# Two decoder layers on one core: one shared pool of buffers, PSUM banks returned earlier, activation tables asked for early, memory keys after the output projection

## The chip, the core and the metric

The kernel runs on one core of one Trainium2 chip. The metric is the device time of one execution in microseconds (us). An engine is named as the profile does: PE is TensorE's matmul side and PEld its weight loads, DVE is VectorE, ACT is ScalarE, POOL is GpSimd, SP is SyncE, which here only issues DMAs.

## What is computed

The reference is a trunk of two decoder layers over 256 tokens of width 1024, in float32. Each layer adds three things to the residual stream x:

```python
x = x + mixer(rms_norm(x, norm_mix[i]), ...)
x = x + memory_cross_attention(rms_norm(x, norm_mem[i]), rms_norm(mem, norm_mem_src[i]), ...)
x = x + swiglu(rms_norm(x, norm_ffn[i]), ffn_w_in[i], ffn_w_out[i])
```

Layer 0's mixer has two groups of eight heads: A selects the top 64 keys of every query by a small indexer, B attends to all causal keys of its block. Layer 1's mixer has 16 heads in 4 groups and three branches (compressed blocks, selected blocks, a window), mixed by gates. Both end in an output projection of 1024 columns. The memory attention has 4 heads of 128 dimensions over 256 memory tokens; its keys are `m @ w_k` of the normed memory and depend on no token of the trunk. The feed-forward part has 2816 hidden columns.

## The kernel before

The 256 tokens are two tiles (t = 0 and 1) of 128 partitions. A float32 product is made of three matmuls in the fp32r format: the operand and the weight are each split into a high part and a rest (`mm3`, L571), so a product over K blocks of 128 rows is 3 K matmuls of up to 512 columns. A weight arrives in units of 256 rows by 512 columns (512 KB) by DMA into one of 3 `raw` buffers; `pusher` (L401) writes its high part (`move`, on ACT or DVE) and its rest (DVE) into one of 6 `whl` buffers, in the fixed order of `plan` (L423 to L444). Each unit serves both token tiles and is then free.

The program has no fixed order of instructions. When it is built, some dozens of generator threads offer instructions, and a list scheduler (`Steps.run`, L108) always issues the one that can start first by its own estimate of the engines' clocks (`Est`, L141), ties within 0.03 us going to the lower rank. So the order on every engine is set at build time by estimated costs, by ranks and by free buffers. A buffer class is a `Slots` object (L269): a thread that wants a buffer waits until one is open. Before the change these classes are separate: 23 `slab`, 4 `t2`, 3 `sn`, 4 `pt`, 2 `gv` (each buffer 2 KB per partition), 2 `t4`, and in PSUM two banks each of `mm`, `sp`, `tp` and `po`.

One thread, `main` (L1502, rank 4, the last in a tie), issues all large products (`gemm`, L577) one after the other: the mixer's input projections, then `mem_k` (L1290, the memory's keys, 48 matmuls), then `project` (L1398, the output projection, 96 matmuls: half 0 for tiles 0 and 1, then half 1), then `mem_attn` (L1315), then `ffn`. Each `gemm` takes one of the two `mm` banks and hands it to an evacuation thread. Most of these call `inv_rms` (L655): ACT squares the bank into a `t2` buffer, DVE sums, POOL takes the inverse root; the caller gives the bank back after that. The attention threads (`attention`, `scores`, L699) run beside `main` at rank 2: two matmuls into an `sp` bank, a masked minimum on DVE into an `sn` buffer, exponentials on ACT, a scaling on POOL or DVE, four transposes into a `tp` bank, a copy into `pt`, and the products with the values into a `po` bank. When a group of eight heads is done for a tile, `finish` (L760) copies it from `po` into two slabs (rows named `slab<-po`), and `project` may use it: it waits for `("oT", t, half)`. `mem_prep` (L1263, rank 2) loads the memory, transposes it and writes it into 8 slabs (rows `slab<-gv`) behind the last projections of the mixer; `mem_k` waits for it.

So what covers the attention's chains on PE is whatever `main` may issue meanwhile. In layer 0 that is the values' projection (`bv`), `mem_k` and `project`; in layer 1 the last query projections, `mem_k` and `project`.

The order of `main` for each layer, before:

```python
            yield from (mixer0 if L == 0 else mixer1)()
            yield from mem_k(L)
            ver += 2
            for t in range(NT):
                spawn(norm(("mem", L), t, 16 + 8 * L, ver))
            yield from project(L)
```

Of the kernel before, what the change touches and what calls it, by code (L numbers as in the profile page):

```python
# [8 lines left out]
F32 = mybir.dt.float32  # L9
# [6 lines left out]
P = 128  # L16
# [37 lines left out]
NSLAB = 23  # L54
TAPS = 8
PTS = 4


class Op:
# [17 lines left out]
    def issue(self):  # L77
        e, outs, ins, cost, f = self.best()[2]
        self.est.issue(e, outs, ins, cost)
        f()  # L80
        for op in self.then:
            op.issue()
# [58 lines left out]
class Est:  # L141


    def __init__(self, nc):
        self.clk = {"PE": 0.0, "V": 0.0, "S": 0.0, "G": 0.0, "D": 0.0, "port": 0.0}
        self.wr, self.rd, self.busy = {}, {}, {}
        self.thin = False
        self.now = 0.0
# [46 lines left out]

    def issue(self, e, outs, ins, cost):
        lock = self.locks(e, outs, ins)
        t = max(self.clk[e], self.after(e, outs, ins), self.clk["port"] if lock else 0.0)
        if e == "PE":
            w = int(t / 3.413)  # L200
            c = cost * (1 if self.busy.get(w - 1, 0.0) > 1.26 else 2)
            n = 1
            for d in outs[0].shape[1:]:
                n *= d
            self.busy[w] = self.busy.get(w, 0.0) + cost * ins[0].shape[0] / P * min(1.0, n / P)
# [14 lines left out]
    class Engine:  # L220
# [3 lines left out]
        def __getattr__(self, name):  # L224
            f = getattr(self.e, name)

            def call(*a, **k):
# [9 lines left out]
                def do():  # L237
                    return f(*a, **{q: v() if q in ("start", "stop") and callable(v) else v for q, v in k.items()})  # L238
                return Op(self.est, [(self.n, outs, ins, self.cost(name, a, k, outs, ins), do)])
            return call  # L240

        def cost(self, name, a, k, outs, ins):
# [56 lines left out]

@with_exitstack  # L300
def trunk(ctx: ExitStack, tc: tile.TileContext, I, out):
# [37 lines left out]
    spawn = ck.spawn  # L339
    MM, SP, TP, PV = Slots(est, pp, "mm", 2), Slots(est, pp, "sp", 2), Slots(est, pp, "tp", 2), Slots(est, pp, "po", 2)  # L340
    SL = Slots(est, hp, "slab", NSLAB)
    T2, T4, SN, PT = Slots(est, tp, "t2", 4), Slots(est, tp, "t4", 2), Slots(est, tp, "sn", 3), Slots(est, tp, "pt", PTS)
    RP = Slots(est, tp, "rope", 3)
    GV = Slots(est, tp, "gv", 2)
# [127 lines left out]
    PO.memset(one, 1.0).issue()  # L472
    mhalf = cp.tile([P, 16], F32, name="mhalf")
# [18 lines left out]
    def tables():  # L492
# [20 lines left out]
        yield S.activation(cos, ang, AF.Sin)  # L513
        yield has(("mix0", 0), 2)
# [254 lines left out]
    def mixer0():  # L769
# [100 lines left out]
        def ev_q(j, key):  # L870
            def ev(ps, free, t):
                q, qf = yield from T2.get([P, 8, HD])
                yield move(q.rearrange("p h d -> p (h d)"), ps)
                yield from inv_rms(ps, 8, HD, (yield from root("mix0", t))[0], 1.0, HD, rq[j, t])
                free()
# [13 lines left out]
        def ev_k(ps, free, t):  # L889
# [3 lines left out]
            yield from inv_rms(ps, 8, HD, (yield from root("mix0", t))[0], 1.0 / HD, 1.0, rk)  # L893
            free()
# [75 lines left out]
        spawn(mem_prep(0), 2)  # L970
# [22 lines left out]
    def mixer1():  # L993
# [92 lines left out]
        def ev_sw(br):  # L1086
            def ev(ps, free, t):
# [4 lines left out]
                yield from inv_rms(ps[:, :256], G, HD, v, 1.0 / HD, 1.0, rk[:, :G])  # L1092
                if br == 0:
                    yield S.activation(vv[:, t, :G, :], ps[:, 256:].rearrange("p (h d) -> p h d", h=G), AF.Copy, scale=r)
                free()
# [28 lines left out]
        def ev_q(j):  # L1124
            def ev(ps, free, t):
                q, qf = yield from T2.get([P, 8, HD])
                yield move(q.rearrange("p h d -> p (h d)"), ps)
                yield from inv_rms(ps, 8, HD, (yield from root("mix1", t))[0], 1.0, HD, rq[j, t])
                free()
# [128 lines left out]
        spawn(mem_prep(1), 2)  # L1258
# [31 lines left out]
    def mem_k(L):  # L1290
# [3 lines left out]
        def ev(ps, free, t):  # L1294
# [3 lines left out]
            yield from inv_rms(ps, MH, MD, mvr[t][0], 1.0 / MD, 1.0, rk)  # L1298
            free()
# [15 lines left out]
    def mem_attn(L):  # L1315
        vm = hp.tile([P, NT, MH, MD], F32, name="mvm")
        qT, rq = {}, [hp.tile([P, MH], F32, name=f"mrq{t}") for t in range(NT)]

        def ev_q(ps, free, t):
            q, qf = yield from T2.get([P, MH, MD])  # L1320
            yield S.activation(q.rearrange("p h d -> p (h d)"), ps, AF.Copy)
            yield from inv_rms(ps, MH, MD, (yield from root(("mem", L), t))[0], 1.0, MD, rq[t])
            free()
# [20 lines left out]
        def mem_pv(t, p, sp, spf, sn, snf):  # L1344
# [20 lines left out]
            for i in range(2):  # L1365
                yield together([T.matmul(po[:, i, :], vm[:, b, h0 + i, :], pt[:, 2 * i + b, :], start=(b == 0), stop=(b == 1))
                                for b in range(2)])
            ptf()
# [191 lines left out]
```

## Time and profile before

| what | us |
|---|---|
| median of 3 runs | 803.68 |
| lowest and highest run | 800.99, 805.22 |
| the profiled execution, its own time | 802.33 |
| its span, from first to last instruction | 800.6 |
| PE busy in the span | 765.6 |
| DVE, ACT, POOL busy | 533.0, 436.7, 132.8 |

The profiled execution's own time is 1.7 us over its span, and 1.35 us under the median. A PE that is shown busy is not always at full rate: a matmul's record reaches over the start of the next, so short waits between matmuls are hidden in it. Line numbers in the trace are all L238, the helper that records every instruction; the rows are told apart by their tiles. `whl` are split weights, `mm`, `sp`, `tp`, `po` the PSUM banks, `t` the buffers of `t2` and `t4`.

### The profile page before, as it was taken

How to read it: one execution, taken by the hardware profiler on the slowest of the kernel's cores; microseconds unless marked ns; L12 is line 12 of the kernel's file. 1: busy time of each engine (PE TensorE's matmuls, PEld its weight loads, DVE VectorE, ACT ScalarE, POOL GpSimd, SP SyncE). 2: the span in 40 equal slices, each digit the busy share in tenths (PEclk: the TensorE clock that was granted, in tenths of full speed). 3: DMA queues.
4: the chain of work that ended last, by engine and by line, in shares of the span. 5: the costliest groups of instructions: out<-in, count | busy, mean ns of one | idle time of the engine just before them, and what ended most of it. 6: DMA issues, size and time to landing. Idle time of an engine off the chain costs nothing.

```text
span 800.6 us, 11834 instructions
## 1 busy us (share of the span) xinstructions
PE 765.6 (96%) x4259; PEld 635.5 (79%) x4259; DVE 533.0 (67%) x1088; ACT 436.7 (55%) x822; POOL 132.8 (17%) x194
## 2 busy tenths in 40 slices
PE   6988999999999999999998988999999999999998
PEld 5766788897888889788877767887897888889886
DVE  6888998868555554554726888886857565546541
ACT  5766985675543443443615677884656344435430
POOL 1665340100000000000016373340200000000000
PEclk9998999999999999999999998999999999999999
DMA  7633643426556645876414623033624665546751
GB/s 221 192 98 92 194 136 100 142 102 193 166 171 206 186 156 157 228 247 186 131 46 123 212 78 106 2 105 108 188 102 132 211 187 183 160 140 212 218 189 52
DMA packets 69482, 121.27 MB, mean 151 GB/s; under 512 B 8420, under 2 KB 15664, under 8 KB 69424
## 3 DMA queue, kind: packets, MB, share of 16 engines
q1 hardware_dynamic: 69392, 120.53, 48.8%
q8 instruction: 33, 0.54, 0.3%
q14 instruction: 25, 0.20, 0.1%
q0 software_dynamic: 32, 0.00, 0.0%
HBM read 119.46 MB, written 1.05 MB: 151 GB/s over the span
## 4 chain that ended last, share of the span: by engine, by line
PE 78%; DVE 8%; ACT 5%; DMA 5%; issue 2%; POOL 1%; SPq 0%; ACTq 0%; DVEq 0%; POOLq 0%
PE mm L238 58%; PE po L238 11%; PE tp L238 7%; PE sp L238 2%; DVE whl L238 2%; DVE slab L238 1%; ACT whl L238 1%; DMA raw<-in_ffn_w_in 1%; DMA raw<-in_ab_w_in 1%; ACT sn L238 1%; DMA raw<-in_nsa_w_in 1%; ACT slab L238 1%; DVE sn L238 1%; DVE kvT L238 1%; DVE hss L238 1%
## 5 line engine op out<-in xcount | busy, mean ns | idle before, releaser
L238 PE MATMUL mm<-whl,h 128*128 128x512 f32 (+3 forms) x1776 | 399.1, 379 | 10.1 <-DVE whl L238 9.1
L238 PEld LDWEIGHTS mm<-whl,h 128*128 128x128 f32 x1776 | 311.8, 189 | 69.9 <-DVE whl L238 10.9
L238 DVE TENSOR_TENSOR whl<-raw,whl 128x1024 fp32r<-128x1024 f32 (+3 forms) x232 | 271.3, 1174 | 143.3 <-ACT whl L238 139.0
L238 ACT ACTIVATE whl<-raw 128x1024 fp32r<-128x1024 f32 (+2 forms) x212 | 214.7, 1016 | 167.4 <-DMA raw<-in_ffn_w_in 42.0
L238 PE MATMUL mm<-whl,slab 128*128 128x512 f32 (+1 forms) x840 | 198.6, 375 | 2.0 <-ACT mvm L238 1.0
L238 PEld LDWEIGHTS mm<-whl,slab 128*128 128x128 f32 x840 | 141.7, 188 | 28.3 <-DVE x L238 1.8
L238 PE MATMUL po<-whl,slab 128*128 128x512 f32 x264 | 68.2, 396 | 0.0
L238 POOL TENSOR_TENSOR rh<-vh,mhalf 128x1 f32<-128x1 f32 x12 | 10.1, 845 | 326.7 <-DVE vh L238 310.5
L238 ACT ACTIVATE slab<-tp 128x256 fp32r<-128x256 f32 (+2 forms) x72 | 31.3, 463 | 50.9 <-PE tp L238 50.8
L238 PEld LDWEIGHTS po<-whl,slab 128*128 128x128 f32 x264 | 49.3, 188 | 11.4
L238 ACT ACTIVATE sn<-sn,mx 128x128 f32<-128x128 f32 (+1 forms) x96 | 42.7, 448 | 6.2 <-DVE mx L238 5.8
L238 POOL TENSOR_TENSOR sn<-sn,rc 128x512 f32<-128x512 f32 (+2 forms) x32 | 32.6, 1022 | 48.9 <-DVE rc L238 30.8
L238 PE MATMUL tp<-ident,t 128*128 128x128 f32 x224 | 35.5, 282 | 4.4 <-DVE slab L238 2.9
L238 PEld LDWEIGHTS tp<-ident,t 128*128 128x128 f32 x224 | 27.3, 143 | 11.8 <-POOL t L238 3.2
L238 DVE CUSTOM_DVE_ANT_0 sn<-sp,cm,rq 128x128 f32<-128x128 f32 (+1 forms) x80 | 30.6, 409 | 7.8 <-PE sp L238 6.6
L238 PE MATMUL tp<-ident,sn 128*128 128x128 f32 (+1 forms) x180 | 31.6, 288 | 2.1 <-POOL sn L238 1.4
L238 ACT ACTIVATE pt<-tp 128x512 f32<-128x512 f32 (+2 forms) x51 | 26.8, 535 | 11.7 <-PE tp L238 11.1
L238 DVE TENSOR_TENSOR x<-mm,x 128x512 f32<-128x512 f32 x36 | 24.5, 686 | 13.0 <-PE mm L238 12.9
L238 ACT ACTIVATE h<-gv 128x512 fp32r<-128x512 f32 x22 | 13.8, 628 | 30.9 <-DVE gv L238 30.9
L238 ACT ACTIVATE t<-mm,rh 128x512 f32<-128x512 f32 (+1 forms) x26 | 17.0, 654 | 24.7 <-PE mm L238 24.7
L238 ACT ACTIVATE t<-mm 128x512 f32<-128x512 f32 (+2 forms) x44 | 23.1, 557 | 9.1 <-PE mm L238 6.9
L238 PEld LDWEIGHTS tp<-ident,sn 128*128 128x128 f32 (+1 forms) x180 | 21.8, 146 | 7.5 <-POOL sn L238 2.3
(198 smaller groups left out, 667.9 us busy)
## 6 DMA issues: line engine op xcount, KB each, us to landing
raw<-in_ffn_w_in SPq DMA_DIRECT2D x80, 512.0 KB, 3.9
raw<-in_ffn_w_out SPq DMA_DIRECT2D x44, 512.0 KB, 4.4
raw<-in_ab_w_in SPq DMA_DIRECT2D x16, 512.0 KB, 3.7
raw<-in_mem_w_kv SPq DMA_DIRECT2D x16, 512.0 KB, 3.8
raw<-in_nsa_w_in SPq DMA_DIRECT2D x16, 512.0 KB, 4.1
raw<-in_ab_w_out SPq DMA_DIRECT2D x8, 512.0 KB, 3.7
raw<-in_mem_w_q SPq DMA_DIRECT2D x8, 512.0 KB, 3.8
raw<-in_mem_w_o SPq DMA_DIRECT2D x8, 512.0 KB, 4.1
```

The costliest lines, as they stand in the source:

```text
L238: return f(*a, **{q: v() if q in ("start", "stop") and callable(v) else v for q, v in k.items()})
```

## The change

The five buffer classes of 2 KB become one pool of 36 places (`Places`, `Kind`). Each class keeps a number of places that nobody else may take (23 slabs, 4 `t2`, 3 `sn`, 2 `pt`, 1 `gv`: 33), and the three that are left go to whoever asks first. The memory's values, before a tile of their own of 4 KB, take two slabs. `inv_rms` is handed the bank's `free` and calls it as soon as the Square is issued, before the sum and the inverse root; in `ev_sw` the copy of the values moves ahead of it. A one-element Sin is issued at the very start on ACT and a one-element Exp right behind the last Sin of `tables`, so that the activation tables are loaded there; the scheduler's estimate now counts 1.28 us for a change of table. `mem_k` and its weights in `plan` move behind `project`, and `mem_prep` gets rank 3. Two estimates change: a matmul of 64 by 64 costs 0.235 us, and the estimate of TensorE's activity counts every matmul in full.

```diff
-NSLAB = 23
+PLACES = 36
+LEAST = {"slab": 23, "t2": 4, "sn": 3, "pt": 2, "gv": 1}
-PTS = 4
...
+    def load(self, func):
+        table = {AF.Sin: "sin", AF.Exp: "exp", AF.Silu: "silu"}.get(func)
+        if table not in (None, self.table):
+            self.table = table
+            self.clk["S"] += 1.28
...
-            self.busy[w] = self.busy.get(w, 0.0) + cost * ins[0].shape[0] / P * min(1.0, n / P)
+            self.busy[w] = self.busy.get(w, 0.0) + cost
...
+                if ins[0].shape[0] == 64 and outs[0].shape[0] == 64:
+                    return 0.235
...
+class Kind:
+    def ready(self):
+        p = self.p
+        if p.used[self.k] < p.least[self.k]:
+            return True
+        return len(p.slots.open) > sum(max(0, p.least[k] - p.used[k]) for k in p.least)
...
+    def ready(func):
+        yield S.activation(warm, one, func)
...
+    places = Places(est, hp, "place", PLACES, LEAST)
+    SL, T2, SN, PT, GV = (places.kind(k) for k in LEAST)
...
-        plan_block((L, "mk"), I["mem_w_kv"][L], 0, 512, KD)
         for half in (0, 1):
             for c in (0, 1):
                 plan_block((L, "out", half, c), ...)
+        plan_block((L, "mk"), I["mem_w_kv"][L], 0, 512, KD)
...
     PO.memset(one, 1.0).issue()
+    S.activation(warm, one, AF.Sin).issue()
...
         yield S.activation(cos, ang, AF.Sin)
+        yield from ready(AF.Exp)
...
-    def inv_rms(ps, H, dh, v, mul, add_k, r):
+    def inv_rms(ps, H, dh, v, mul, add_k, r, free):
         sq, f = yield from T2.get([P, H, dh])
         yield S.activation(sq.rearrange("p h d -> p (h d)"), ps, AF.Square)
+        free()
...
-        spawn(mem_prep(0), 2)
+        spawn(mem_prep(0), 3)
...
-        spawn(mem_prep(1), 2)
+        spawn(mem_prep(1), 3)
...
-        vm = hp.tile([P, NT, MH, MD], F32, name="mvm")
+        vm = {}
...
+                if p == 0:
+                    vm[t] = yield from SL.get([P, MH, MD])
...
             yield from (mixer0 if L == 0 else mixer1)()
-            yield from mem_k(L)
             ver += 2
             for t in range(NT):
                 spawn(norm(("mem", L), t, 16 + 8 * L, ver))
             yield from project(L)
+            yield from mem_k(L)
```

## Rows read from the trace of the kernel before

**Rows 1.** The page: the span, the engines' busy time, the chain that ended last.

```profile
span 800.6 us, 11834 instructions
...
PE 765.6 (96%) x4259; PEld 635.5 (79%) x4259; DVE 533.0 (67%) x1088; ACT 436.7 (55%) x822; POOL 132.8 (17%) x194
...
PE 78%; DVE 8%; ACT 5%; DMA 5%; issue 2%; POOL 1%; SPq 0%; ACTq 0%; DVEq 0%; POOLq 0%
```

**Rows 2.** Busy time by stage: stretch, its length, engines, clock, DMA share, GB/s.

```profile
40.00:90.00 50.00, 42.61 (x217) 33.50 (x216) 44.39 (x130) 34.67 (x72) 25.33 (x41) 0.93 0.40 119
90.00:180.00 90.00, 90.00 (x598) 76.70 (x597) 75.88 (x182) 65.73 (x150) 20.09 (x18) 1.00 0.41 126
...
380.00:460.00 80.00, 74.89 (x473) 61.51 (x472) 48.77 (x96) 40.17 (x76) 24.36 (x41) 1.00 0.43 127
460.00:500.00 40.00, 33.43 (x265) 28.51 (x264) 32.92 (x123) 30.43 (x95) 21.84 (x29) 0.87 0.28 94
500.00:562.00 62.00, 61.94 (x458) 51.58 (x457) 50.55 (x158) 44.06 (x117) 16.71 (x20) 1.00 0.22 69
```

**Rows 3.** The same view in stretches of 10 us, around the fallen clock.

```profile
60.00:70.00 10.00, 7.97 (x45) 6.54 (x43) 7.42 (x18) 5.78 (x11) 4.40 (x7) 1.00 0.54 157
70.00:80.00 10.00, 8.09 (x33) 5.97 (x34) 9.70 (x32) 6.32 (x14) 5.78 (x10) 0.66 0.10 25
...
480.00:490.00 10.00, 8.37 (x66) 7.40 (x65) 7.52 (x24) 5.78 (x17) 3.22 (x4) 0.66 0.63 211
```

**Rows 4.** The chain in order of time, one piece at full rate: start, us, what.

```profile
198.60 13.76 PE mm L238 x60
```

**Rows 5.** ACT's timeline, two of its six table loads and what follows one.

```profile
21.63 1.28 ACT L238 ACT_TABLE_LOAD   x1
22.92 0.22 ACT L238 ACTIVATE sin<-ang 128x16 f32<-128x16 f32 x1
...
83.64 1.28 ACT L238 ACT_TABLE_LOAD   x1
```

**Rows 6.** ACT's timeline: the copy and the Square of two `mm` banks, layer 0.

```profile
35.94 0.59 ACT L238 ACTIVATE t<-mm 128x512 f32<-128x512 f32 x1
...
45.58 0.61 ACT L238 ACTIVATE t<-mm 128x512 f32<-128x512 f32 x1
...
60.63 0.60 ACT L238 ACTIVATE t<-mm 128x512 f32<-128x512 f32 x1 [1.82 <-PE mm L238]
...
65.49 0.59 ACT L238 ACTIVATE t<-mm 128x512 f32<-128x512 f32 x1
```

**Rows 7.** PE's timeline: the second `bk` product; what stands ahead of the first `bv`.

```profile
47.11 3.83 PE L238 MATMUL mm<-whl,h 128*128 128x512 f32 x16
...
70.21 0.91 PE L238 MATMUL tp<-ident,t 128*128 128x128 f32 x4 [2.24 <-DVE slab L238]
70.77 1.63 PE L238 MATMUL mm<-whl,h 128*128 128x512 f32 x3
```

**Rows 8.** Attention stretches, columns of rows 2: all, then `whl`, then `mm` (twice) alone.

```profile
94.40:108.30 13.90, 13.90 (x86) 11.46 (x86) 13.84 (x38) 12.15 (x28) 7.35 (x6) 1.00 0.50 152
...
94.40:108.30 13.90, 10.03 (x38) 6.25 (x36) 5.19 (x5) 4.18 (x5) 1.00 0.50 152
...
108.30:134.50 26.20, 16.72 (x55) 9.77 (x56) 2.06 (x3) 1.09 (x2) 1.00 0.31 87
...
498.70:545.00 46.30, 23.49 (x78) 13.61 (x79) 1.38 (x2) 2.26 (x4) 1.00 0.15 47
```

**Rows 9.** DVE's timeline: the attention's results written for `project`, three of eight.

```profile
107.63 0.68 DVE L238 TENSOR_TENSOR slab<-po,slab 128x512 fp32r<-128x512 f32 x1
...
490.12 0.69 DVE L238 TENSOR_TENSOR slab<-po,slab 128x512 fp32r<-128x512 f32 x1 [0.16 <-ACT slab L238]
...
544.26 0.69 DVE L238 TENSOR_TENSOR slab<-po,slab 128x512 fp32r<-128x512 f32 x1 [0.97 <-ACT slab L238]
```

**Rows 10.** PE's timeline: the first matmul of layer 1's memory keys.

```profile
498.69 0.72 PE L238 MATMUL mm<-whl,slab 128*128 128x512 f32 x2
```

More of the change, by code (lines that the diff above doesn't have):

```diff
@@ L78, in issue @@
         e, outs, ins, cost, f = self.best()[2]
+        if e == "S":
+            self.est.load(getattr(f, "func", None))
         self.est.issue(e, outs, ins, cost)
@@ L147, in __init__ @@
         self.thin = False
+        self.table = None
         self.now = 0.0
@@ L238, in do @@
                     return f(*a, **{q: v() if q in ("start", "stop") and callable(v) else v for q, v in k.items()})
+                do.func = a[2] if self.n == "S" else None
                 return Op(self.est, [(self.n, outs, ins, self.cost(name, a, k, outs, ins), do)])
@@ L297, in get, with __init__, kind, take @@
         return self.take(shape, dt)
+class Places:
+    def __init__(self, est, pool, name, n, least):
+        self.slots, self.least, self.used = Slots(est, pool, name, n), least, dict.fromkeys(least, 0)
+    def kind(self, k):
+        return Kind(self, k)
+class Kind:
+    def __init__(self, places, k):
+        self.p, self.k = places, k
+    def ready(self):
[3 more added lines that the diff above has]
+        return len(p.slots.open) > sum(max(0, p.least[k] - p.used[k]) for k in p.least)
+    def take(self, shape, dt=F32):
+        self.p.used[self.k] += 1
+        t, f = self.p.slots.take(shape, dt)
+        def free():
+            f()
+            self.p.used[self.k] -= 1
+        return t, free
+    def get(self, shape, dt=F32):
+        yield self.ready
+        return self.take(shape, dt)
 @with_exitstack
@@ L873, in ev @@
                 yield move(q.rearrange("p h d -> p (h d)"), ps)
-                yield from inv_rms(ps, 8, HD, (yield from root("mix0", t))[0], 1.0, HD, rq[j, t])
-                free()
+                yield from inv_rms(ps, 8, HD, (yield from root("mix0", t))[0], 1.0, HD, rq[j, t], free)
                 yield from rope(q, 8, ra[:, t, 2 * j], rb[:, t, 2 * j], HALF)
@@ L892, in ev_k @@
             rk = tiny(8, "rk8")
-            yield from inv_rms(ps, 8, HD, (yield from root("mix0", t))[0], 1.0 / HD, 1.0, rk)
-            free()
+            yield from inv_rms(ps, 8, HD, (yield from root("mix0", t))[0], 1.0 / HD, 1.0, rk, free)
             yield from rope(q, 8, ra[:, t, 3], rb[:, t, 3], HALF)
@@ L1127, in ev @@
                 yield move(q.rearrange("p h d -> p (h d)"), ps)
-                yield from inv_rms(ps, 8, HD, (yield from root("mix1", t))[0], 1.0, HD, rq[j, t])
-                free()
+                yield from inv_rms(ps, 8, HD, (yield from root("mix1", t))[0], 1.0, HD, rq[j, t], free)
                 quT[t, j] = yield from SL.get([P, 4, P])
@@ L1297, in ev @@
             rk = tiny(MH, "mrk")
-            yield from inv_rms(ps, MH, MD, mvr[t][0], 1.0 / MD, 1.0, rk)
-            free()
+            yield from inv_rms(ps, MH, MD, mvr[t][0], 1.0 / MD, 1.0, rk, free)
             yield V.tensor_tensor(q, q, rk[:, :, None].to_broadcast([P, MH, MD]), op=OP.mult)
@@ L1321, in ev_q @@
             yield S.activation(q.rearrange("p h d -> p (h d)"), ps, AF.Copy)
-            yield from inv_rms(ps, MH, MD, (yield from root(("mem", L), t))[0], 1.0, MD, rq[t])
-            free()
+            yield from inv_rms(ps, MH, MD, (yield from root(("mem", L), t))[0], 1.0, MD, rq[t], free)
             qT[t] = (yield from SL.get([P, MH, P], F32R)), (yield from SL.get([P, MH, P], F32R))
@@ L1365, in mem_pv @@
             for i in range(2):
-                yield together([T.matmul(po[:, i, :], vm[:, b, h0 + i, :], pt[:, 2 * i + b, :], start=(b == 0), stop=(b == 1))
+                yield together([T.matmul(po[:, i, :], vm[b][0][:, h0 + i, :], pt[:, 2 * i + b, :], start=(b == 0), stop=(b == 1))
                                 for b in range(2)])
             ptf()
+            done(("mpv", L))
+            if has(("mpv", L), 2 * NT)():
+                for b in range(NT):
+                    vm[b][1]()
             hl, hf = yield from SL.get([P, 2, 2, P], F32R)
```

14 lines of the change are left out of this document (5 added, 9 removed).

## The prediction

> **What bounds the kernel now.** I read the page first. PE is busy for 765.6 of 800.6 us and 78% of the chain that ended last is PE's own work [rows 1]. So the kernel is bound by PE, and only two things can shorten it: idle time of PE, 800.6 - 765.6 = 35.0 us, and time in which its clock was not granted in full.
>
> Next I cut the span into stages. From 90 to 180 us PE is busy throughout. Two pockets hold what the change can reach: 40 to 90 us (layer 0's projections and indexer), where PE is idle for 50 - 42.6 = 7.4 us, and 460 to 500 us (layer 1's attention with no large product beside it), idle for 40 - 33.4 = 6.6 us [rows 2]. From 380 to 460 us another 5.1 us are idle, and from 500 to 562 us nothing [rows 2]. In both pockets the clock falls as well: the granted share averages 0.93 and 0.87 [rows 2], because in some stretches TensorE ran at 1.2 instead of 2.4 GHz, as the mean of 0.66 in two stretches of 10 us shows; ahead of the first, from 60 to 70 us, PE had been busy for 7.97 of 10 us [rows 3]. The lost clock is worth at most 0.07 x 50 = 3.5 us and 0.13 x 40 = 5.2 us. So the first pocket holds 10.9 us at most, the second 11.8 us. What else could hold them open is DVE: it is busy for 44.4 of the 50 us and 32.9 of the 40 us [rows 2], so with its work unchanged the pockets cannot shrink by more than 5.6 and 7.1 us. Last I took a price for cover: a product's matmul of 512 columns takes 13.76 / 60 = 0.229 us at the full rate [rows 4].
>
> **The change part by part.**
>
> *Tables.* A load takes 1.28 us on ACT and Sin's stands at 21.63 us, in the middle of the first weight splits [rows 5]. With Sin asked for first, its load takes the place of the one that opens the program, and Exp's moves from 83.64 us to right behind the last cosine, still in the first splits. So ACT loses one load near the start and one at 83.64 us, and gains one near the start, where it waits for weights part of the time. One load is saved outright; I take -1.3 us, with ends 0 (the new Exp load costs in the start what Sin's did, and DVE hides the other) and -2.6 us (two loads, the new one hidden).
> At 21.63 us the load ends at 22.91 and the Sin starts at 22.92 us [rows 5], so no wait beside the 1.28 us shows. The Trainium skill (ScalarE: Activation LUTs, What ACT_TABLE_LOAD costs) counts a drain of about 1.38 us more for each switch; by it this part would be worth -2.7 and the whole sum 1.4 us lower; the trace does not bear the drain out.
>
> *Banks and places, layer 0.* The second `aq` bank is copied at 35.94 us but squared only at 45.58 us, and the first `bq` bank is copied at 60.63 and squared at 65.49 us [rows 6]. The Square wants a second `t2` buffer and the four are held by tiles that wait for their rotation. The next product in that bank begins behind it, at 47.11 and 70.77 us [rows 7]. In the second case the bank was also returned only with the inverse root; PE's order then had transposes ahead of the product, and PE sat idle for 2.24 us before one of them [rows 7]; the fallen clock of 70 to 80 us follows [rows 3]. Three free places give the Square its buffer, and the earlier return puts the product ahead of that wait. What then is late is DVE: it is busy for 9.70 us of 70 to 80 us [rows 3]. I take -4 us: the 2.24 us and about half of the clock's 3.4 us there. Ends: 0, since DVE may hold everything as it is, and DVE's -5.6 us.
>
> *Keys behind the projection, layer 0.* Nothing is added or removed: two products, their evacuation, 4 weight units with their DMAs on SP, split on ACT and DVE, all move behind 96 matmuls. SP's loads stay in the order of use and its queue passes no other kind. But the cover changes hands. `mem_k` waits for no attention, `project` does: it now stands next in `main`, and everything behind it waits too. Before, 38 matmuls on `mm` filled 94.4 to 108.3 us, 38 x 0.229 = 8.7 us of 13.9, until the first result lay ready at 107.63 + 0.68 = 108.3 us [rows 8, 9]. That cover is gone: PE has attention alone there. On the other hand DVE is full in that stretch (13.84 of 13.9 us), 5.19 us of it weight splits [rows 8], which now stop once six units stand ready; and `mem_prep` steps back in rank. So the first result comes earlier. Count by matmuls: before, 38 + 55 = 93 matmuls were through by 134.5 us, when the last result was ready [rows 8]; now only 72 may be (half 0, and half 1 for tile 0). The other 21 x 0.229 = 4.8 us come after. If attention, freed of half of these 5.19 us of splits, ends 2.8 us sooner, +2 us remain. I take +2; ends +8.7 (the whole cover, nothing sooner) and -1 us (all splits and some of the memory's evacuation out of the way).
>
> *Layer 1.* Here the old order had a hole: the first matmul of the keys comes at 498.69 us [rows 10], since `mem_prep` wanted 8 slabs while keys, queries and results held nearly all 23. `project` can start at 490.12 + 0.69 = 490.8 us, when the first result is ready [rows 9]: 8 us sooner. But by count 78 matmuls on `mm` started between 498.7 and 545.0 us [rows 8], where the last result is ready (544.26 + 0.69) [rows 9]; now 72 may, so 6 x 0.229 = +1.4 us come later. What may gain is attention's own speed: it has three `sn` buffers, one of them held by the compressed branch, and now up to six; splits and keys' evacuation leave it alone. I take -4.5 us, about two fifths of the pocket's 11.8, since DVE caps it at 7.1; ends 0 and -7.1. Together -3.1 us.
>
> *The rest.* `pt` falls from four assured buffers to two, `gv` from two to one; the values' tile becomes two slabs. Nothing is idle on PE from 500 to 562 us, where these classes are used most [rows 2], so they cost 0; if slabs take all free places, `pt` may cost PE up to +1 us. In the output projection's wake nothing needs the keys at once: the queries' two products, 48 x 0.229 = 11 us, still stand between. The new estimates only reorder; their place is 380 to 460 us, so between -5.1 us of idle time and as much the other way; I take 0.
>
> Sum: -1.3 - 4 + 2 - 3.1 = -6.4 us. The profiled execution took 802.33 us, so 795.9; it lies 1.35 us under the median of 803.68, so about **797 us** as a median.
>
> **Rivals.**
>
> *Slower: the lost cover in layer 0 decides.* `project` waits for A's first result, and if that comes hardly sooner, PE has about 14 us of attention alone: +8.7 us. PE then works 13.9 - 8.7 = 5.2 of 13.9 us, a smaller share than ahead of the fall at 70 us, so the clock would fall too; a stretch like 480 to 490 us costs 3.4 us [rows 3]. With layer 1's +1.4 us, tables at -1.3 and banks at -4 us that is +8.2: about 812 us. It decides once the waits after `bv` exceed what tables, banks and layer 1's attention give, 1.3 + 4 + 3.1 = 8.4 us. For it: PE is full from 90 to 180 us [rows 2], so nothing there can get better. Against: DVE's full load there, a third of it splits [rows 8].
> The Trainium skill (TensorE: Matmul & The Clock Gate, What's actually happening) says that the throttled clock is the default and activity lifts it, which speaks against taking cover away; the 0.66 stretches agree.
>
> *No change: the pockets belong to DVE.* Banks given back sooner then only move PE's wait to the next split of weights, and `mem_prep`'s slabs take the three free places in layer 1, so `sn` stays at three: the pool does not do what it says. Left are -1.3 + 2 + 1.4 and a microsecond or two of gain: 802.5 us. For it: 9.70 us of DVE in 70 to 80 us [rows 3]. Against: 2.24 us idle behind a bank, not a split [rows 7].
>
> *Much faster.* Both pockets shrink to DVE's limit and layer 0's cover is neutral: -2.6 - 5.6 - 7.1 + 1.4 = -13.9: about 789 us or less.
>
> **How the numbers follow.** A measurement of this kernel can tell some 0.5%, 4 us, from no change. Forecast 0.45 and much faster 0.10, together 0.55 faster; no change 0.28; slower 0.17. The likeliest case's own range is 791 to 799.5 us. The range of 8 in 10 goes from 786 (a little past DVE's limit) to 809 us, short of the full price of the lost cover.
>
> **What would show it.** Right: five table loads, two before 30 us; the Squares of [rows 6] within 2 us of their copies; a granted share near 1 from 60 to 80 us; layer 0's first result well before 108 us; the output projection's first matmul in layer 1 before 490 us, and PE idle less than 5 us in that pocket. Wrong: PE idle behind `bv` for several us with a clock under 1, Squares still late, or layer 1's attention as long as before; then the time is 803 or more.

## The result, and the profile after

The changed kernel takes 794.81 us (median of 4 runs, 793.35 to 795.79), beside 802.77 us for the kernel before on the same chip (800.99 to 805.22): a ratio of 0.9897, with an interval of [0.9865, 0.993]. The profiled execution took 795.09 us, its span is 793.4 us. The sum of the prediction gave 795.9 us for that. The total is right, but by luck: several of its terms are wrong, and the errors cancel.

The page of the changed kernel, the lines that answer to [rows 1]:

```profile
span 793.4 us, 11801 instructions
...
PE 761.5 (96%) x4259; PEld 632.1 (80%) x4259; DVE 531.4 (67%) x1085; ACT 430.8 (54%) x819; POOL 146.2 (18%) x201
```

PE's idle time is 793.4 - 761.5 = 31.9 us, against 35.0 us. So of the 7.2 us by which the span is shorter 3.1 us are idle time. PE's busy time fell by the other 4.1 us, with the same number of matmuls: less time at half clock (the mean granted clock is 0.998, before 0.989) and fewer short waits hidden in matmul records look like that.

Busy time by stage, columns as in [rows 2]:

```profile
40.00:90.00 50.00, 43.09 (x230) 33.99 (x228) 45.80 (x120) 32.44 (x64) 33.28 (x40) 1.00 0.43 127
90.00:180.00 90.00, 85.84 (x556) 71.98 (x557) 76.14 (x188) 61.69 (x147) 23.72 (x23) 0.98 0.38 123
380.00:460.00 80.00, 76.25 (x479) 62.35 (x478) 47.56 (x93) 40.09 (x76) 26.75 (x45) 1.00 0.45 134
460.00:500.00 40.00, 38.13 (x348) 32.90 (x347) 36.91 (x166) 37.40 (x128) 24.98 (x31) 1.00 0.24 80
500.00:562.00 62.00, 62.00 (x420) 51.34 (x420) 49.27 (x123) 42.36 (x98) 14.66 (x17) 1.00 0.38 119
84.00:102.00 18.00, 11.99 (x84) 9.62 (x85) 17.93 (x81) 14.15 (x47) 7.71 (x10) 0.91 0.17 59
...
70.00:80.00 10.00, 8.18 (x44) 6.20 (x43) 9.86 (x24) 6.72 (x12) 7.58 (x6) 1.00 0.52 158
90.00:100.00 10.00, 7.96 (x52) 5.95 (x52) 10.00 (x43) 8.98 (x30) 5.00 (x6) 0.83 0.17 52
```

Layer 1's pocket (460 to 500 us) has all but closed: 1.87 us idle, clock 1.00. Layer 0's fallen clock at 70 us is gone too (1.00). But from 90 to 180 us, where PE had no idle microsecond [rows 2], it now has 4.2. The row for 84 to 102 us shows where: PE works for 12 of 18 us while DVE is full (17.93 us), and from 90 to 100 us the clock falls to 0.83. That is the lost cover of which the prediction's first rival spoke.

PE's timeline of the changed kernel (start, us, what, idle time ahead and what ended it):

```profile
79.02 4.85 PE L245 MATMUL mm<-whl,h 128*128 128x512 f32 x20
84.79 0.85 PE L245 MATMUL tp<-identr,t 128*128 128x128 f32 x8 [0.92 <-DVE t L245]
...
88.81 0.72 PE L245 MATMUL sp<-place,place 128*128 128x256 f32 x4 [2.15 <-DVE mx L245]
...
102.37 0.71 PE L245 MATMUL mm<-whl,place 128*128 128x512 f32 x2
104.63 0.71 PE L245 MATMUL sp<-place,place 128*128 128x256 f32 x4 [1.55 <-DVE mx L245]
...
152.19 2.00 PE L245 MATMUL mm<-whl,h 128*128 128x512 f32 x8
...
496.87 1.18 PE L245 MATMUL mm<-whl,place 128*128 128x512 f32 x4
```

The values' product ends at 83.9 us; the next matmul on `mm`, the output projection's first, comes at 102.37 us, and PE waits in between for one of DVE's masked minima (2.15 us) and for another behind it (1.55 us). At 152.19 us the memory's queries begin. What the projection waits for, the attention's results in DVE's timeline, lines that answer to [rows 9]:

```profile
101.57 0.69 DVE L245 TENSOR_TENSOR place<-po,place 128x512 fp32r<-128x512 f32 x1
...
126.20 0.68 DVE L245 TENSOR_TENSOR place<-po,place 128x512 fp32r<-128x512 f32 x1
...
485.03 0.68 DVE L245 TENSOR_TENSOR place<-po,place 128x512 fp32r<-128x512 f32 x1
...
526.47 0.68 DVE L245 TENSOR_TENSOR place<-po,place 128x512 fp32r<-128x512 f32 x1
```

Layer 0's first result is ready at 102.3 us instead of 108.3, its last at 126.9. Layer 1's last is ready at 527.2 us. Layer 1's first is ready at 485.7 us, yet the projection starts at 496.87, 11 us later. PE was busy for 10.32 of the 11.2 us from 485.7 to 496.9, with scores, transposes and products with the values; what putting the projection ahead of them would do was not tried. Columns of [rows 8], `mm` alone, from the projection's first matmul to the attention's last result:

```profile
102.30:126.90 24.60, 12.28 (x43) 7.53 (x44) 2.04 (x3) 0.00 (x0) 1.00 0.35 109
496.80:527.20 30.40, 11.10 (x39) 6.66 (x40) 1.49 (x3) 0.00 (x0) 1.00 0.11 36
```

Last ACT's timeline, lines that answer to [rows 5] and [rows 6]:

```profile
0.79 1.28 ACT L245 ACT_TABLE_LOAD   x1 [0.79 <-PEq L1604]
...
24.87 1.28 ACT L245 ACT_TABLE_LOAD   x1
26.16 0.20 ACT L245 ACTIVATE warm<-one 128x1 f32<-128x1 f32 x1
...
59.80 1.08 ACT L245 ACTIVATE place<-mm 128x512 f32<-128x512 f32 x2
```

There are five loads, two of them before 30 us, and copy and Square of the first `bq` bank now stand together (x2 at 59.80 us), where 4.9 us lay between them before.

### The profile page after: what moved, and what is told of

Same layout as the page of the kernel before. It is cut to its first block, busy times and chain, and to the rows that moved or that the text cites. A ratio compares the mean times of both kernels' runs of the same rounds, so it can differ in the third digit from the quotient of the medians.

```text
span 793.4 us, 11801 instructions
## 1 busy us (share of the span) xinstructions
PE 761.5 (96%) x4259; PEld 632.1 (80%) x4259; DVE 531.4 (67%) x1085; ACT 430.8 (54%) x819; POOL 146.2 (18%) x201
## 4 chain that ended last, share of the span: by engine, by line
PE 75%; DVE 9%; DMA 7%; ACT 5%; issue 2%; SPq 1%; POOL 1%; ACTq 0%; DVEq 0%; POOLq 0%
PE mm L245 56%; PE po L245 9%; PE tp L245 7%; DMA raw<-in_ffn_w_out 4%; DVE whl L245 3%; PE sp L245 3%; ACT place L245 3%; DVE place L245 2%; ACT whl L245 2%; DMA raw<-in_nsa_w_in 1%; DVE kvT L245 1%; DMA x<-in_x 1%; DMA raw<-in_ffn_w_in 0%; DVE x L245 0%; DVE m L245 0%
## 5 line engine op out<-in xcount | busy, mean ns | idle before, releaser
L245 ACT ACTIVATE whl<-raw 128x1024 fp32r<-128x1024 f32 (+3 forms) x209 | 211.5, 1014 | 161.1 <-DMA raw<-in_ffn_w_out 46.7
L245 PE MATMUL mm<-whl,place 128*128 128x512 f32 (+1 forms) x840 | 193.2, 373 | 1.6 <-DVE x L245 1.2
L245 PEld LDWEIGHTS mm<-whl,place 128*128 128x128 f32 x840 | 142.1, 188 | 28.7 <-DVE x L245 2.1
L245 ACT ACTIVATE place<-tp 128x512 f32<-128x512 f32 (+4 forms) x124 | 57.6, 491 | 62.7 <-PE tp L245 62.4
L245 PE MATMUL po<-whl,place 128*128 128x512 f32 x264 | 68.1, 395 | 0.0
L245 PEld LDWEIGHTS po<-whl,place 128*128 128x128 f32 x264 | 49.3, 188 | 11.4
L245 PE MATMUL tp<-ident,place 128*128 128x128 f32 (+1 forms) x340 | 53.3, 278 | 3.5 <-POOL place L245 1.8
L245 PEld LDWEIGHTS tp<-ident,place 128*128 128x128 f32 (+1 forms) x340 | 39.6, 142 | 13.7 <-POOL place L245 3.1
L245 ACT ACTIVATE place<-place,mx 128x128 f32<-128x128 f32 (+1 forms) x96 | 42.8, 450 | 8.7 <-DVE mx L245 8.3
L245 POOL TENSOR_TENSOR place<-place,rc 128x512 f32<-128x512 f32 (+2 forms) x35 | 32.4, 930 | 28.6 <-DVE rc L245 20.0
L245 DVE TENSOR_TENSOR x<-mm,x 128x512 f32<-128x512 f32 x36 | 24.4, 683 | 12.0 <-PE mm L245 11.9
```

## The experiments

The theory was that layer 0 pays for the lost cover and would be some us faster with the keys first, that the places carry layer 1's gain, and that banks and tables are worth 2 to 5 and 1 to 2.5 us. The rivals were that DVE sets layer 0's end in any order, so that the order costs nothing there, and that order and banks carry the gain.

The ratio of each kernel is to the kernel before on the same chip (medians 801.43, 802.27 and 802.63 us); the changed kernel's 0.9897 is the mark. One table carries most of the readings. It cuts the profiled execution of each kernel at the first matmul on `mm` of a large product, found by counting the matmuls in the order of `main`: the start up to layer 0's `bk`; layer 0 from there to the memory's queries (indexer, attention, projection, keys); the middle up to layer 1's `kc`; from `kc` to `q0`; layer 1 from `q0` to its memory's queries; the end.

| kernel | ratio to before | start | layer 0 | middle | kc to q0 | layer 1 | end |
|---|---|---|---|---|---|---|---|
| before | 1 | 35.6 | 112.6 | 236.9 | 54.0 | 122.6 | 238.9 |
| changed | 0.9897 [0.9865, 0.993] | 35.2 | 117.0 | 238.4 | 49.2 | 115.1 | 238.5 |
| keys_first_layer0 | 0.9922 [0.9893, 0.995] | 34.5 | 116.3 | 239.7 | 49.2 | 114.2 | 238.3 |
| keys_first_both | 1.008 [1.0058, 1.0103] | 35.2 | 117.0 | 238.4 | 49.2 | 127.0 | 238.4 |
| own_pools | 0.9986 [0.9965, 1.0008] | 35.0 | 118.3 | 236.9 | 48.7 | 120.1 | 238.3 |
| banks_late | 0.9931 [0.9905, 0.9957] | 34.7 | 117.8 | 239.4 | 50.7 | 113.2 | 238.5 |
| keys_first_l0_rank2 | 0.9842 [0.9827, 0.9858] | 35.3 | 112.1 | 239.0 | 49.2 | 113.8 | 238.7 |
| keys_first_both_rank2 | 0.9882 [0.9865, 0.99] | 35.5 | 112.6 | 237.3 | 49.2 | 117.4 | 239.8 |
| own_pools_sn6 | 0.9866 [0.9852, 0.9881] | 35.1 | 115.8 | 236.7 | 48.5 | 113.7 | 240.4 |
| no_warm | 0.9994 [0.9979, 1.0008] | 36.1 | 119.1 | 239.5 | 50.7 | 115.1 | 238.7 |
| l0_first_no_warm | 0.9884 [0.9863, 0.9906] | 37.8 | 110.2 | 240.5 | 50.7 | 115.2 | 238.8 |
| l0_first_sn6 | 0.9819 [0.9797, 0.9841] | 34.5 | 111.9 | 236.1 | 48.6 | 113.8 | 240.3 |
| before_sn6 | 1.0043 [1.0028, 1.0058] | 38.4 | 112.8 | 239.2 | 54.0 | 120.0 | 240.1 |
| before_order | 1.0035 [1.0018, 1.0052] | 36.8 | 118.3 | 237.3 | 54.0 | 117.5 | 238.5 |

Two executions of one order of instructions differ too. Up to layer 0's `bk`, no_warm and l0_first_no_warm have the same order on every engine and take 36.1 and 37.8 us; in the middle keys_first_l0_rank2 and keys_first_both_rank2 do, with 239.0 and 237.3; in layer 0 the changed kernel and banks_late do, with 117.0 and 117.8. So a stage difference under 2 us is not read by itself. The stage from `kc` to `q0` is steadier: five kernels with the same order there all take 49.2 us.

**The keys ahead of the projection, rank 3 kept.** In layer 0 alone, then in both layers (`L in (0, 1)`):

```diff
+        if L in (0,):
+            plan_block((L, "mk"), I["mem_w_kv"][L], 0, 512, KD)
         for half in (0, 1):
...
             yield from (mixer0 if L == 0 else mixer1)()
+            if L in (0,):
+                yield from mem_k(L)
...
             yield from project(L)
-            yield from mem_k(L)
+            if not (L in (0,)):
+                yield from mem_k(L)
```

> The changed kernel, with the memory's keys (and their weights) ahead of the output projection again in layer 0 alone; layer 1 keeps them behind it. Theory (lost cover): in the changed kernel layer 0 takes 68.7 us from the last values' matmul to the first memory query against 54.0 us before, with PE idle for 4.2 us and half clock in it; with the keys back as cover this falls to some 57 us, so about 11 us come off the changed kernel's 794.8: 784 us (781 to 788). Rival (the stretch is DVE's): attention ends sooner because the keys' work is out of its way, so putting it back gives little: 791 to 796 us.

> The changed kernel, with the keys ahead of the output projection in both layers, as before the change; the shared places, the banks and the tables stay. Theory (layer 1's 12 us come from the shared places, not from the order): the same as with the keys back in layer 0 alone, within 3 us: 781 to 788 us. Rival (the order is what freed layer 1's attention): layer 1 loses at least half of its 12 us again, 6 us or more above the kernel with the keys back in layer 0 alone: 790 us or more.

The first is no faster than the changed kernel (the intervals overlap); its 795.12 us lie in the rival's range. PE's timeline says why, at the first matmul of the keys' second tile:

```profile
116.64 1.79 PE L245 MATMUL mm<-whl,place 128*128 128x512 f32 x7
```

`main` stood at that product until 116.64 us, because at rank 3 the memory's preparation came behind the attention; only one of the two products covered anything. So this run does not test the cover. In both layers it is slower than the changed kernel by 1.008 - 0.9897 = 0.0183, 14.7 us; the two profiled executions differ by 11.9, all of it in layer 1 (127.0 against 115.1 us). SP's timeline, the load of the memory's second tile; then PE's timeline, the first `mm` matmul since 475.85 us; then the busy time:

```profile
500.29 0.46 SPq L1319 DMA_DIRECT2D t<-in_mem  x1
```

```profile
521.81 1.41 PE L245 MATMUL mm<-whl,place 128*128 128x512 f32 x5
```

```profile
500.00:562.00 62.00, 53.52 (x367) 43.88 (x368) 40.90 (x108) 31.66 (x77) 11.07 (x14) 0.97 0.25 85
```

`main` waited for the memory; when its keys could start, the attention was nearly done (last result 525.7 us), keys and projection were all still to do, and PE was idle for 8.5 us.

**The same with the old rank.** On top of the edit above; the second line pair in the second kernel alone, which so undoes order and rank and nothing else:

```diff
-        spawn(mem_prep(0), 3)
+        spawn(mem_prep(0), 2)
...
-        spawn(mem_prep(1), 3)
+        spawn(mem_prep(1), 2)
```

> The changed kernel with the keys ahead of the output projection in layer 0 and the memory's preparation there back at rank 2; layer 1 stays changed. With rank 3 the second tile of keys had waited 24 us for its memory, so the cover was only half there. Theory (lost cover): with the memory in time, both key products fill PE from 83 us on and layer 0 ends 4 to 8 us sooner: 787 to 791 us (ratio 0.981 to 0.986). Rival (layer 0 is DVE's from 40 to 100 us): the memory's five or six us on DVE stand in front of the selection again, the first result comes at 106 us or later, and nothing is gained: 793 to 797 us (ratio 0.988 to 0.993).

> The changed kernel with order and rank both undone: keys ahead of the output projection and the memory's preparation at rank 2 in both layers; shared places, banks and tables stay. Theory (the order alone cost layer 1 its 13 us, through the wait for the memory's slabs): still 5 us or more above the kernel with the keys first in layer 0 alone: 798 us or more (ratio 0.994 or more). Rival (the rank did it: at rank 3 the memory came too late for keys that stand first): 790 to 796 us (ratio 0.985 to 0.992), and layer 1's first key product starts near 499 us as in the old kernel.

The first is faster than the changed kernel, 0.9842 against 0.9897 with intervals that do not meet; layer 0 takes 112.1 instead of 117.0 us. The rows of keys_first_l0_rank2, busy time and PE's timeline:

```profile
84.00:102.00 18.00, 15.92 (x89) 12.81 (x88) 18.00 (x71) 12.88 (x32) 6.19 (x7) 1.00 0.37 120
```

```profile
84.36 0.93 PE L245 MATMUL mm<-whl,place 128*128 128x512 f32 x3
```

The keys begin at 84.36 us, right behind the values; PE works 15.92 us in the stretch where it worked 11.99, at full clock, although DVE is as full as before. So the cover was worth 4.9 us. The second is as fast as the changed kernel within the intervals, the rival's time: of what the new order costs in layer 0 (117.0 against 112.6) it gives back about half in layer 1 (115.1 against 117.4). So no gain of the order as a whole shows. In layer 1 the keys first are bad mainly with rank 3: with rank 2 the first `mm` matmul comes at 505.46 instead of 521.81 us (not near 499, as the rival had it), and the stage takes 117.4 instead of 127.0. PE's and DVE's timelines of keys_first_both_rank2, this matmul and the attention's last result:

```profile
505.46 0.50 PE L245 MATMUL mm<-whl,place 128*128 128x512 f32 x1
...
522.17 0.68 DVE L245 TENSOR_TENSOR place<-po,place 128x512 fp32r<-128x512 f32 x1
```

**The old buffer classes.** The old sizes, with the values in a tile of their own; then fixed classes with the room that the change made given to `sn`:

```diff
-    places = Places(est, hp, "place", PLACES, LEAST)
-    SL, T2, SN, PT, GV = (places.kind(k) for k in LEAST)
+    SL = Slots(est, hp, "slab", 23)
+    T2, SN, PT, GV = Slots(est, tp, "t2", 4), Slots(est, tp, "sn", 3), Slots(est, tp, "pt", 4), Slots(est, tp, "gv", 2)
...
-        vm = {}
+        vmt = hp.tile([P, NT, MH, MD], F32, name="mvm")
+        vm = {t: (vmt[:, t], lambda: None) for t in range(NT)}
...
-                if p == 0:
-                    vm[t] = yield from SL.get([P, MH, MD])
```

For own_pools_sn6 the line of the classes has `sn` 6, `pt` 2 and `gv` 1. With the values' own tile of 4 KB it holds 4 KB more than the changed kernel.

> The changed kernel with the five buffer classes separate again (23 slabs, 4 t2, 3 sn, 4 pt, 2 gv and the values' own tile); order, banks and tables stay changed. Theory (the places carry layer 1): its attention is back to three score buffers and takes about 10 us longer, and layer 0's Squares wait for t2 buffers again, some 3 us: 804 to 812 us. Rival (the order and the banks carry it): 0 to 3 us more: 795 to 798 us.

> The changed kernel with fixed classes again, but the three free places given to the score buffers for good: 23 slabs, 4 t2, 6 sn, 2 pt, 1 gv. Theory (layer 1's attention was short of score buffers): it keeps the gain of the shared places, 792 to 797 us (ratio 0.988 to 0.993), and layer 1's attention is as quick as in the changed kernel. Rival (the free places served t2 or the slabs): no better than with the old classes, 799 to 803 us (ratio 0.997 to 1.001).

Without the places nearly the whole gain is gone: 0.9986, 7.1 us above the changed kernel, between the theory's range and the rival's. The two profiled executions differ by 3.9 us, and layer 1 alone by 5.0 (120.1 against 115.1 us). Its pocket, in own_pools:

```profile
460.00:500.00 40.00, 34.90 (x318) 30.20 (x317) 37.80 (x140) 34.57 (x111) 17.63 (x21) 1.00 0.30 99
```

Five us idle, where the changed kernel has 1.87. With six fixed `sn` the stage takes 113.7 us and the ratio is 0.9866: as good as the shared places, and by the overlap of the intervals not shown to be better. So what the places give layer 1 is score buffers; that they are shared adds nothing that shows here.

**The banks returned late.** In `inv_rms`, `free()` moves from behind the Square to behind the inverse root:

```diff
         yield S.activation(sq.rearrange("p h d -> p (h d)"), ps, AF.Square)
-        free()
...
         yield from pow_half(r, ss)
+        free()
```

> The changed kernel with the PSUM banks returned only behind the inverse root, as before the change; the rest stays changed. Theory: the first product of the values in layer 0 again comes behind the transposes that wait, and the narrow products of layer 1 (kw, vw) wait for their banks again: 2 to 5 us more, 797 to 800 us. Rival (with the shared places the Square comes early enough and the return was only an order on paper): within 1.5 us of 794.8.

The ratios differ by 2.7 us, but their intervals overlap: by the time it can't be told from the changed kernel. Moreover every engine has the same order of instructions in both kernels up to 428 us. So in layer 0 the late return changes nothing, and what differs there is one execution from another. It is not little: the row of banks_late shows PE busy for 13.79 us at a clock of 0.72, where the changed kernel had 11.99 at 0.91:

```profile
84.00:102.00 18.00, 13.79 (x82) 11.85 (x83) 17.40 (x80) 13.67 (x47) 6.99 (x9) 0.72 0.13 50
```

Behind 428 us the late return costs 1.5 us from `kc` to `q0`, and layer 1 took 113.2 us, no more than in the changed kernel. So the banks carry little of the gain.

**The tables not asked for early.** Both one-element activations and the estimate's 1.28 us for a load go; once on the changed kernel, once on keys_first_l0_rank2:

```diff
-        if e == "S":
-            self.est.load(getattr(f, "func", None))
...
-    S.activation(warm, one, AF.Sin).issue()
...
-        yield from ready(AF.Exp)
```

> The changed kernel without the two early table loads and without their estimate; all else stays changed. Theory: one load more on ACT, 1.28 us, in the first splits of the start, and Exp's again in the first scores: 1 to 2.5 us more, 796 to 797.5 us (ratio 0.991 to 0.993). Rival (DVE and the DMAs hide it): within 1 us of the changed kernel.

> The kernel with the keys first in layer 0 (rank 2 there), now without the two early table loads and their estimate. Without them the changed kernel had lost 7.7 us, with half clock for 13.7 us behind the values' product. Theory (the loads themselves are worth about 1.3 us, the rest was a clock that fell because that stretch had no cover): here, with cover, the loads cost 1 to 2.5 us: ratio 0.985 to 0.988, clock 1.00 from 60 to 120 us. Rival (the late loads push the whole schedule back by several us wherever they stand): ratio 0.990 or more.

On the changed kernel it costs 0.9994 - 0.9897 = 0.0097, or 7.8 us, six times what I took, and beyond the theory's range and the rival's. Its busy time from 40 us on:

```profile
40.00:90.00 50.00, 44.31 (x230) 35.85 (x229) 44.15 (x120) 33.48 (x62) 28.54 (x42) 0.94 0.37 118
84.00:102.00 18.00, 13.17 (x66) 10.52 (x68) 17.32 (x64) 13.88 (x39) 8.22 (x10) 0.62 0.26 88
90.00:150.00 60.00, 55.30 (x343) 43.33 (x343) 49.95 (x140) 40.98 (x111) 19.48 (x20) 0.93 0.34 112
```

Exp's load falls at 88.43 us, into the stretch that has lost its cover, and there TensorE gets 0.62 of its clock: for much of it 1.2 GHz. Where the keys cover that stretch, the same removal costs 0.9884 - 0.9842 = 0.0042, 3.4 us, with the load at 88.19 us in the same place; the row of l0_first_no_warm:

```profile
84.00:102.00 18.00, 13.55 (x77) 10.44 (x78) 17.50 (x68) 13.68 (x34) 3.68 (x7) 1.00 0.36 117
```

PE works hardly more here, but at full clock, and it has that from 60 to 120 us, as the theory said; the ratio of 0.9884 lies between the theory's range and the rival's. Up to the memory's queries the removal costs 155.2 - 152.2 = 3.0 us without cover and 148.0 - 147.4 = 0.6 us with it. How much of the two prices the cover decides stays rough: by the intervals of the ratios I estimate them as 7.8 give or take 2.9 and 3.4 give or take 2.2 us, the two pairs of profiled executions differ by 5.9 and 5.0 us, and a clock in this stretch is not firm in one execution (0.91 and 0.72 for the same order, above). Firmer is the mean granted clock, which is on record for every run: 0.986 to 0.994 in ten runs of no_warm against 0.995 to 0.998 in four of the changed kernel, and 0.993 to 0.999 against 1.0 with the cover. So more lost clock goes with the missing early loads; that a load brings the clock down is not shown.

**Parts alone in the kernel before, and the best version.** The edit of before_sn6, on the kernel before:

```diff
-PTS = 4
+PTS = 2
...
-    T2, T4, SN, PT = Slots(est, tp, "t2", 4), Slots(est, tp, "t4", 2), Slots(est, tp, "sn", 3), Slots(est, tp, "pt", PTS)
+    T2, T4, SN, PT = Slots(est, tp, "t2", 4), Slots(est, tp, "t4", 2), Slots(est, tp, "sn", 6), Slots(est, tp, "pt", PTS)
...
-    GV = Slots(est, tp, "gv", 2)
+    GV = Slots(est, tp, "gv", 1)
```

The edit of before_order, on the kernel before:

```diff
-        plan_block((L, "mk"), I["mem_w_kv"][L], 0, 512, KD)
         for half in (0, 1):
...
+        plan_block((L, "mk"), I["mem_w_kv"][L], 0, 512, KD)
         plan_block((L, "mq"), I["mem_w_q"][L], 0, 512, KD)
...
-        spawn(mem_prep(0), 2)
+        spawn(mem_prep(0), 3)
...
-        spawn(mem_prep(1), 2)
+        spawn(mem_prep(1), 3)
...
-            yield from mem_k(L)
...
             yield from project(L)
+            yield from mem_k(L)
```

l0_first_sn6 has the edits of keys_first_l0_rank2 and own_pools_sn6 together.

> The kernel before, with one thing changed: six score buffers in place of three, two pt in place of four and one gv in place of two, so the same memory. Order, banks, tables and ranks are the old ones. Theory (score buffers are what layer 1's attention lacked): layer 1 from its first to its memory queries takes 164 to 170 us in place of 176.5, ratio 0.986 to 0.992. Rival (it is the sharing, with t2 or slabs taking places, or the order): ratio 0.996 or more.

> The kernel before, with one thing changed: the keys and their weights behind the output projection in both layers and the memory's preparation at rank 3. Classes, banks and tables are the old ones. Theory (layer 0 loses its cover, some 4 us; layer 1 gains some 3 us or nothing while attention is short of score buffers): ratio 0.999 to 1.010, 0.0 to 8 us slower. Rival (the order is a gain of its own): ratio 0.996 or less.

> The two kernels that did best put together: keys first in layer 0 at rank 2, and fixed classes with six score buffers (23 slabs, 4 t2, 6 sn, 2 pt, 1 gv, the values' own tile). Theory (two causes in two places, layer 0's cover and layer 1's score buffers, which add up): ratio 0.980 to 0.983, 786 to 789 us. Rival (in layer 0 the shared places are what lets the memory through in time, so with fixed classes the cover comes late): ratio 0.985 to 0.989.

Alone, either part makes the old kernel slower by about 3 us. before_sn6 gains 2.6 us in layer 1 and loses 2.8 at the start and 2.3 in the middle; which of its three sizes costs that was not tried. Its layer 1 from `kc` takes 54.0 + 120.0 = 174.0 us, so the theory's 164 to 170 were missed. The layer 1 pocket of before_sn6:

```profile
460.00:500.00 40.00, 35.27 (x307) 30.61 (x307) 38.01 (x152) 35.27 (x112) 23.73 (x29) 1.00 0.38 122
```

It closed by less than 2 us, where the same six buffers close it to 1.77 us in l0_first_sn6:

```profile
460.00:500.00 40.00, 38.23 (x375) 33.11 (x374) 38.56 (x171) 37.04 (x131) 18.78 (x25) 1.00 0.24 80
```

The attention itself is nearly as quick in before_sn6 as in the changed kernel; what is late is `main`. PE's and DVE's timelines of before_sn6, the keys' first matmul and the last result:

```profile
516.17 0.48 PE L238 MATMUL mm<-whl,slab 128*128 128x512 f32 x1
...
533.68 0.68 DVE L238 TENSOR_TENSOR slab<-po,slab 128x512 fp32r<-128x512 f32 x1
```

Counted from `q0`, its last result comes after 89.8 us (105.8 in the kernel before, 87.4 in the changed one), but its keys begin after 71.6 us (59.5 in the kernel before). before_order, as forecast, gains 5.1 us in layer 1 and loses 5.7 in layer 0. l0_first_sn6 is the best kernel of the study: 788.91 us, 0.9819, its interval clear of the changed kernel's. That it beats keys_first_l0_rank2 is not shown, the intervals overlap.

## Why the prediction was right, and where it was not

The sum had -6.4 us; the ratio gives 0.0103 x 802.77 = -8.3. By stages the changed kernel stands at -0.4 (start), +4.4 (layer 0), +1.5 (middle), -4.8 (`kc` to `q0`), -7.5 (layer 1) and -0.4 us (end), together -7.2. The prediction had -3.3 in layer 0 with the tables, -3.1 in layer 1, and 0 elsewhere.

**Layer 0, the order: sign right, size short.** I took +2 us; runs that undo it measure 4.4 to 4.9, and the order alone in the old kernel 5.7. The step that failed is "now only 72 may be": only 43 matmuls were through by the last result at 126.9 us, since no matmul of half 1 started before 128.2 us. Against 93 before, that is 50 x 0.229 = 11.5 us to come after, not 4.8. The gain was underrated as well: counted from the stage's start the last result came 98.9 - 91.7 = 7.2 us sooner, not 2.8. 11.5 - 7.2 = +4.3, what the stage shows; the clock of 0.83 is in it. So the first rival's mechanism did act, cover lost and a fallen clock behind the values, at about half of its 8.7 us; my "wrong" sign for it came true while the time was right. The Trainium skill (TensorE: Matmul & The Clock Gate, What's actually happening) says that activity lifts the throttle; the 0.91 from 84 to 102 us, and the 1.00 of the same stretch with the keys in it, agree.

**Layer 0, banks and places: the leads came, worth little.** I took -4 us. The second `bk` product starts at 43.8 instead of 47.1 us, `bv` at 65.9 instead of 70.8, the values' product ends some 11 us sooner, and the fallen clock at 70 us is gone. The earlier return of the banks is not needed for this, since banks_late has the same order here. The lead of `bk` is the places' (46.84 us in own_pools), but `bv` starts at 65.44 us there too, so either the banks or the places would do for it alone, or the changed estimates moved it; no run tells. Nor does the lead arrive at the stage's end. With the old order and rank (keys_first_both_rank2) layer 0 takes 112.6 us, as before; undone singly, the banks change nothing in this stage, and the places' 1.3 us are less than two executions of one order can differ by. The step that failed is taking the value next to the row of the 2.24 us wait, instead of the end at 0 that was named with it, "DVE may hold everything as it is": DVE is busy for 17.93 and 18.00 of the 18 us in both orders, and 45.80 us of 40 to 90, more than before. That DVE is the cause is the reading that fits; no run took work from DVE.

**Layer 1, places: right.** -4.5 us predicted, -5.0 measured (own_pools), and -6.4 with six fixed `sn`. It is attention's own speed, as the step said: from `q0` to the last result it takes 102.4 us in own_pools and 87.4 in the changed kernel. In the old kernel six `sn` alone gave that speed as well, but only 2.6 us of the stage.

**Layer 1, the order: wrong sign.** I took +1.4 us; it gives 2.3 to 3.6 us in the new kernel, 5.1 in the old. The same count failed here: 39 matmuls were through, not 72, so 39 x 0.229 = 8.9 us more than before come after. But the last result came at 527.2 us instead of 545.0, counted from `q0` 18.4 us sooner; of that 8.9 were given back, and some 2 us more on the way to the queries. In the new kernel that speed is the places', as I had booked it: with the order undone (keys_first_both_rank2) the last result comes 88.2 us after `q0` against 87.4. What the order (with its rank) moves there is `main`'s next product. With the keys first it begins 70.8 us after `q0`, with the projection first 57.1, and by the last result 29 of its matmuls have started instead of 39: 10 x 0.229 = 2.3 us, what the stages show. So the step that failed compared with the 78 matmuls of the old kernel, where a slow attention left more time for them. The ratios of keys_first_l0_rank2 and keys_first_both_rank2, which differ by the order and rank of layer 1 alone, give 3.2 us with intervals that do not meet. In the old kernel the order alone also made the attention itself quicker, 98.2 instead of 105.8 us; what the keys bring along (8 slabs, evacuations, splits) may have held it up, and which of the three, no run tells. The projection's start before 490 us did not come (496.87), and was not needed.

**Tables: too small by far.** I took -1.3 us with ends 0 and -2.6; it is 7.8 us in the changed kernel and 3.4 in a covered one. The step that failed prices the loads by their own 1.28 us. What goes beyond them is in part lost clock: by the medians of the runs' mean clocks, 0.996 against 0.991, some 0.005 x 799 = 4 us, an estimate. 1.5 us more stand from `kc` to `q0`, where the order of instructions is another one without the early loads. How a load brings this about no run shows. Both removals took out the estimate of 1.28 us as well; which of the two counts was not tried. The load does end without a drain here: it ends at 24.87 + 1.28 = 26.15 us, and the Exp starts at 26.16. The Trainium skill's 1.38 us for one (ScalarE: Activation LUTs, What ACT_TABLE_LOAD costs) is not borne out.

**The rest: 0 taken, -4.8 us found from `kc` to `q0`.** All three kernels on the old program take 54.0 us there, all others 48.5 to 50.7. It is neither the places (own_pools 48.7) nor the order (49.2); late banks and unasked tables cost 1.5 us each. PE's idle time from 415 to 440 us went from 25 - 21.23 = 3.8 to 25 - 24.55 = 0.45 us, the rows of before and after the change:

```profile
415.00:440.00 25.00, 21.23 (x139) 18.86 (x139) 16.83 (x42) 12.87 (x30) 15.66 (x30) 1.00 0.42 122
415.00:440.00 25.00, 24.55 (x170) 21.21 (x166) 13.96 (x37) 13.63 (x32) 18.37 (x33) 1.00 0.36 101
```

For the rest the two changed estimates and the copy of the values in `ev_sw`, which every run on the changed kernel kept ahead of the Square, are left as causes. None was run alone: open.

One price of the rivals does not follow from its terms: -1.3 + 2 + 1.4 us less a microsecond or two of gain, on the median of 803.68, is 803.8 to 804.8 us and not 802.5.

So the forecast case came true in its total, by two errors that cancel: layer 0 about 7 us worse than forecast, layer 1 and the stretch ahead of it about 9 us better. "Much faster" was the truth for layer 1's pocket, "no change" for layer 0's, "slower" for layer 0's order.

## What to carry to other kernels

When a product moves behind another, count not how many of its matmuls may be issued by the last result, but what the fixed order behind it lets through, and ask separately when the product that now comes first can start, and how long the chain that it covers will last. The same move cost 5 us in one layer and gave 2 to 5 in the other: decide such an order stage by stage. And try the rank or priority of the feeder together with the order: with the wrong one the old order looked 15 us worse than the new, with the right one it was equal. And before a stage's difference is read, look whether the two kernels differ in it at all: two executions of one order differed by up to 1.7 us.

## What was not expected of the hardware

The granted clock does not follow from a stretch's busy time, as the prediction's first rival took it to: from 84 to 102 us PE was busy for 13.17 us at 0.62 in no_warm, 13.79 at 0.72 in banks_late, and 13.55 at 1.00 in l0_first_no_warm. Nor does it follow from the order of the instructions, which is the same there in banks_late and in the changed kernel with its 0.91. And two parts each look worth nearly the whole gain when taken out (7.1 us for the places, 7.8 for the tables, of 8.3 in all), while six score buffers, which do what the places do for layer 1, cost 3 us when put into the old kernel alone: a gain by removal is not a share of the sum. The tables were not put in alone.
